# An S5/RWKV-7 layer: S5's second tables and phases on ScalarE, one scan per batch, block masks first in the queue

## The chip, the cores and the metric

The kernel runs on one core of a Trainium2 chip. The metric is the time of one execution in microseconds (us), measured on the device. The engines are called as in the profile: PE (TensorE, matmuls), DVE (VectorE), ACT (ScalarE), POOL (GpSimd), SP (SyncE, which issues most DMAs).

## The reference

One layer of a hybrid decoder, for 1024 tokens of width 1024, all in float32:

```
h    = rms_norm(x);  proj = h @ w_in
# columns: RWKV r, k, v (3 x 512), low-rank downs, S5 input u (512), two gates
o_rwkv = rwkv7_branch(...) @ w_branch_rwkv      # 8 heads of 64, a state per head, token by token
o_s5   = s5_branch(u, ...) @ w_branch_s5
x = x + rms_norm((sigmoid(gA) * o_rwkv + sigmoid(gB) * o_s5) @ w_out)
x = x + rms_norm(conv_ffn(rms_norm(x)))         # gated MLP with a causal convolution of width 3

# S5: 32 groups of 16 channels, 64 complex states per group
a_bar = exp(lam * dt);  b_bar = ((a_bar - 1) / lam) * b
s_t   = a_bar * s_(t-1) + b_bar u_t             # along the tokens
y     = Re(c s) + d u;  then gelu and a sigmoid gate

# RWKV-7: the state S of a head, per token
S = S * w + (S a) b^T + v k^T;   y = S r        # a = -kk, b = kk * sigmoid(..)
```

## The kernel before

**Products.** A float32 product is split: each operand is a rounded part and a remainder, and three matmuls of 128x512 (L172, L173, L174) give hi*hi, lo*hi and hi*lo for each k tile of 128. A weight tile is loaded by SP (wf, L155), rounded on ACT (wh, L156), and its remainder is made on DVE (wl, L157).

**Order of the work.** PE's order is the order in which the program emits its matmuls. `drive` (L179) runs lanes: generators that yield what their PE work costs and when (or on what condition) they may go on. When no lane is due, `background` emits a step of the projections in the fill list (input projections, r, k and v, gates), whose matmuls fill PE while the lanes' small operations run elsewhere. The order on the other engines comes from a scheduler that takes instructions by priority: the lanes' number (HP, the more urgent HP2, and HPW, more urgent still, which weight loads and projections have).

**S5 stage** (`drive` at L1785, lanes `s5_lane` and `tab_lane`). The 32 groups are worked in 4 batches of 8 groups; time is cut into 128 blocks of 8 tokens, so a batch's tiles are 128 partitions x 8 groups x 128 blocks (the 128 partitions hold the real part of the 64 states in one half, the imaginary part in the other). `s5_tables(b)` (L492) makes the tables of a batch from step powers: the input side bb, bw, bx (small tiles of 128x128; `lin` is two products and a sum, L508 to L510), from bw and bx the table w, and the output side ca and cb (`tab`, L529; sums at L532 and L537). w is transposed on PE (L544) and copied (L545, L546); the short convolution kpad is multiplied on PE (L553), copied (L554) and unrolled into toep by 8 DMAs (L562). Then it makes the phases: block number times frequency, in a high and a low part fh and fl (L569, L572), reduced by whole turns (L570, L571, L574, L575), and then |x| (L576) and two sines (L577, L578), which give the cosine cs and the sine sn.

`s5_batch(b)` (L583) multiplies the input by the transposed table into two PSUM tiles p1, p2 (L598), turns them by cs and sn (L600 to L602), runs along the blocks the recurrence z = rho * z + rot with one scan per group (L605, 8 scans of 127 columns, each from zero), turns the state (L607, L608), and PE adds three products per group: toep with u (L613), ca with z (L614), cb with rot (L615). The PSUM tiles called chk, two in number, serve all of L544, L553, L598 and L613 to L615. A copy (L616) and a DMA end the batch. All wide tiles come from one pool (t4).

**RWKV stage** (`drive` at L1795ff, four lanes). Heads are worked in pairs; a front (`rwkv_front`, L639) takes the two pairs u = 0, 1 of a group g for one half th of the tokens. `prep_lane(0)` and `prep_lane(1)` run the fronts g = 0 (here "the first front") and g = 1 ("the second front") of each token half; with g = 1 the inverses follow. A front loads k, tz, ta, r, v (L654, from a pool `ld` of ten tiles); squares k (L669) and scans the decay (L673); makes bk1 (L674, L675); sums the squares on PE (L680) into a tile of the PSUM pool rp, which has two; from these the inverse square (L684, L685) and yb (L686); the exponentials pe and tz (L690, L691); the operands ar0, bk0 (L693 to L695); transposes yb on PE into kb (L700); bk0, ar1, r and bk1 (L703 to L706); and then, for each pair and each half q of its eight chunks, 16 block products on PE (L718, 64x128) into two of the four PSUM buffers cz, which two multiplications by a mask empty into gr (L721). L725 makes the bonus product, L730 and L737 DMA the results out on POOL's queue. `rwkv_nat` (L740) transposes bk (L747) and v (L762) and copies them on ACT (L754, L756, L767); its eight-fold V copies free rp. `chain_lane` then runs the level (L822) and the chain.

The second front of a half begins when the first has masked its first pair (`masked`), and its own instructions go on when T_LD has passed (`start`), in the second token half for g = 0 when the first chain is done.

## Time and profile before

| | |
|---|---|
| three runs | 1543.03, 1545.65, 1549.22 us (median 1545.65) |
| the profiled execution | 1545.26 us |
| its span, first to last instruction | 1543.5 us, so 1.8 us lie around it |
| granted PE clock, mean over the span | 0.974 |
| busy: PE / DVE / ACT / POOL | 1455.5 / 1084.8 / 696.9 / 74.0 us |
| S5 stage | about 84 to 262 us |
| first two RWKV fronts | about 262 to 345 us |
| fronts of the second token half | about 500 to 560 us |

A row of the waits names the waiting instruction's output and line, the instruction that released it, and the sum, the number and the longest of these waits. A row of the groups names line, engine, operation, output and input with their shapes, then busy time and mean ns, then the idle time in front of them. A timeline row has start, length, engine, line and operation, and in brackets the idle time before it with its releaser. In the windows the granted clock is the share of full speed that the throttle gave PE in that stretch.

### The profile page before, as it was taken

Reading aid. Unit: us, or ns where it says so; the run is one execution under the profiler, and the core shown is the slowest. Engines: PE = TensorE matmul, PEld = TensorE weight load, DVE = VectorE, ACT = ScalarE, POOL = GpSimd, SP = SyncE. Lnnn points to the kernel's source line nnn. Section 1 sums busy time; section 2 is a strip of 40 time slices with the busy share of each in tenths; the row PEclk is TensorE's granted clock in tenths of the full one; section 3 lists DMA queues with packets and bytes.
Section 4 is the critical chain, followed back from the end, with each engine's and each line's share of the span. In section 5 each row is a group of like instructions: output and inputs, shape, how many; then the busy total and the mean of one; then the engine's idle time right before and its main releaser. Section 6 shows DMA issues by size and latency. Waiting matters only on the chain.

```text
span 1543.5 us, 24191 instructions
## 1 busy us (share of the span) xinstructions
PE 1455.5 (94%) x9332; PEld 1191.3 (77%) x9332; DVE 1084.8 (70%) x1783; ACT 696.9 (45%) x1077; POOL 74.0 (5%) x126
## 2 busy tenths in 40 slices
PE   5999899999999899899898999999999999999996
PEld 4788788778777677678676888788888887888785
DVE  6898784845325748466587689777777777698777
ACT  5364442533324535436444446444444444443451
POOL 2100000001100010000100000000000000000001
PEclk9999999999999899999998999999999999999998
DMA  6164242623511475424864444322222225953632
GB/s 209 42 205 126 87 127 100 206 88 117 158 57 63 152 225 161 119 79 132 269 217 153 151 144 133 111 83 82 82 82 82 82 85 195 335 169 114 214 109 109
DMA packets 130339, 210.45 MB, mean 136 GB/s; under 512 B 37696, under 2 KB 43840, under 8 KB 130224
## 3 DMA queue, kind: packets, MB, share of 16 engines
q1 hardware_dynamic: 122480, 185.17, 37.4%
q0 software_dynamic: 6592, 21.64, 4.1%
q10 hardware_dynamic: 1152, 2.10, 0.4%
q8 instruction: 73, 1.20, 0.3%
q14 instruction: 42, 0.34, 0.1%
HBM read 153.28 MB, written 53.48 MB: 134 GB/s over the span
## 4 chain that ended last, share of the span: by engine, by line
PE 76%; DVE 10%; DMA 6%; ACT 4%; issue 3%; SPq 0%; POOL 0%; ACTq 0%; DVEq 0%; POOLq 0%
PE gm L172 9%; PE gm L173 8%; PE gm L174 8%; PE rp L1384 4%; PE d L1559 4%; PE d L1558 4%; PE rp L1385 4%; PE rp L1386 4%; PE d L1560 4%; PE mm L1384 2%; PE mm L1386 2%; PE mm L1385 2%; PE ch L172 1%; PE ch L173 1%; PE ch L174 1%
## 5 line engine op out<-in xcount | busy, mean ns | idle before, releaser
L172 PE MATMUL gm<-hh,wh 128*128 128x512 f32 x688 | 282.8, 411 | 11.1 <-DVE hl L1116 5.8
L173 PE MATMUL gm<-hl,wh 128*128 128x512 f32 x688 | 271.9, 395 | 0.2 <-DVE hl L227 0.2
L174 PE MATMUL gm<-hh,wl 128*128 128x512 f32 x656 | 258.4, 394 | 0.0
L156 ACT CAST wh<-wf 128x512 fp32r<-128x512 f32 x179 | 110.8, 620 | 225.0 <-PE gm L173 138.0
L157 DVE TENSOR_TENSOR wl<-wf,wh 128x512 fp32r<-128x512 f32 x175 | 120.2, 688 | 120.6 <-ACT wh L156 112.7
L172 PEld LDWEIGHTS gm<-hh,wh 128*128 128x128 f32 x688 | 130.8, 190 | 45.1 <-DVE hl L1116 7.5
L173 PEld LDWEIGHTS gm<-hl,wh 128*128 128x128 f32 x688 | 130.9, 190 | 25.7 <-issue 1.0
L174 PEld LDWEIGHTS gm<-hh,wl 128*128 128x128 f32 x656 | 124.9, 190 | 27.3
L1559 PE MATMUL d<-xl,wh 128*128 128x512 f32 x308 | 120.8, 392 | 3.0 <-DVE xl L227 3.0
L1558 PE MATMUL d<-xh,wh 128*128 128x512 f32 x308 | 121.1, 393 | 2.4 <-ACT xh L226 2.1
L1560 PE MATMUL d<-xh,wl 128*128 128x512 f32 x308 | 120.5, 391 | 0.0
L1384 PE MATMUL rp<-t,h 128*128 128x512 f32 x216 | 84.4, 391 | 1.4 <-ACT p L1398 1.4
L1386 PE MATMUL rp<-t,l 128*128 128x512 f32 x216 | 84.2, 390 | 0.5 <-DVE l L227 0.5
L1385 PE MATMUL rp<-t,h 128*128 128x512 f32 x216 | 84.1, 389 | 0.0
L1558 PEld LDWEIGHTS d<-xh,wh 128*128 128x128 f32 x308 | 58.2, 189 | 15.9 <-ACT xh L226 2.5
L1559 PEld LDWEIGHTS d<-xl,wh 128*128 128x128 f32 x308 | 58.2, 189 | 15.8 <-DVE xl L227 3.9
L1560 PEld LDWEIGHTS d<-xh,wl 128*128 128x128 f32 x308 | 58.2, 189 | 12.3
L226 ACT CAST h<-r 128x1024 fp32r<-128x1024 f32 x34 | 35.9, 1054 | 61.1 <-PE rp L1385 32.5
L227 DVE TENSOR_TENSOR l<-r,h 128x1024 fp32r<-128x1024 f32 x34 | 41.6, 1225 | 29.2 <-ACT h L226 27.7
L1405 DVE SCALAR_TENSOR_TENSOR y<-zv,vecs,y 128x1023 f32<-128x1023 f32 (+1 forms) x36 | 46.1, 1281 | 8.5 <-ACT y L1403 8.5
L1384 PEld LDWEIGHTS rp<-t,h 128*128 128x128 f32 x216 | 40.5, 188 | 10.8 <-ACT p L1398 2.2
L1386 PEld LDWEIGHTS rp<-t,l 128*128 128x128 f32 x216 | 40.5, 188 | 9.4 <-DVE l L227 1.0
(462 smaller groups left out, 3201.3 us busy)
## 6 DMA issues: line engine op xcount, KB each, us to landing
r<-in_w_up_dram SPq DMA_DIRECT2D x36, 512.0 KB, 3.6
wf<-in_w_in_dram SPq DMA_DIRECT2D x68, 256.0 KB, 2.9
st<-in_w_down_dram SPq DMA_DIRECT2D x55, 256.0 KB, 4.2
st<-ACT SPq DMA_DIRECT2D x44, 256.0 KB, 4.8
wf<-in_w_up_dram SPq DMA_DIRECT2D x36, 256.0 KB, 2.6
ACT<-y POOLq DMA_DIRECT2D x18, 512.0 KB, 2.9
GT<-ev SPq DMA_DIRECT2D x32, 256.0 KB, 2.4
wf<-in_w_br_dram SPq DMA_DIRECT2D x32, 256.0 KB, 3.4
```

What stands on the lines that cost most here:

```text
L156: nc.scalar.copy(h[:, :n], f[:, :n])
L157: nc.vector.tensor_tensor(l[:, :n], f[:, :n], h[:, :n].bitcast(F32), ALU.subtract)
L172: mm(ps, a, xh[k], start=k == 0, stop=False)
L173: mm(ps, a, xl[k], start=False, stop=False)
L174: mm(ps, b, xh[k], start=False, stop=k == n - 1)
L1384: mm(ps, wh[:, c], xh, start=first and k == 0, stop=False, skip_group_check=True)
L1385: mm(ps, wh[:, c], xl, start=False, stop=False, skip_group_check=True)
L1386: mm(ps, wl[:, c], xh, start=False, stop=k == 3, skip_group_check=True)
L1405: V.scalar_tensor_tensor(y[:, lag:], z[:, 0:1024 - lag], self.vec(nme, i), y[:, lag:], ALU.mult, ALU.add)
L1558: mm(ps, wh[:, c], xh[:, x], start=start, stop=False, skip_group_check=True)
L1559: mm(ps, wh[:, c], xl[:, x], start=False, stop=False, skip_group_check=True)
L1560: mm(ps, wl[:, c], xh[:, x], start=False, stop=stop, skip_group_check=True)
```

## The change

1. **Second tables.** bx and cb are bw and ca with the two halves of the partitions exchanged and one of them negated. They are now made so on ACT, two instructions each (64 partitions each); the six DVE operations per batch that made them from the inputs go, and one tile (ct2) with them.
2. **Phases.** The two 1024-wide DVE products of block number and frequency become 16 ACT activations of 128x128 with a scale per partition. After the sines, ph is filled with rho (an ACT copy) and its column 0 of every group with zero (a POOL memset), and is kept for the scan.
3. **One scan.** The turned input is written one column to the right, with column 0 zero, and one scan of 1024 columns runs over all eight groups; the zeros of ph restart it at each group.
4. **Priorities in S5.** `s5_lane` gets HP2 for HP.
5. **Fronts.** The exponentials move ahead of the first yield, the -0.5 goes into yb, and ar0, ar1, r * bk1, bk1 * tz, tz * k and bk0 are made before the kb transposes, so that one operation per pair stands behind them. The number of operations stays. T_BK is 4 for 5.
6. **Masks and the second front.** The masks get priority HPW. A counter `grams` counts fronts whose block products are all emitted; the second front's own instructions wait for that of the first (`grams > 2 * th`) in place of T_LD, and prep_lane(1) starts only when the last projection of r, k, v has begun (`all_in`).

PE has 6405 rows of instructions before and after, SP 703; DVE 1719 for 1752, ACT 1053 for 1025, POOL 111 for 106. PE's order is the same up to the first RWKV front.

In the S5 stage, batch 0, before, on ACT (t tiles: phase, sine and cosine; ev: evictions of projections; wh: weight casts):

```order
L1015 ACTIVATE ev_1416<-gm_1403,hb_a_217 128x512
L156 CAST wh_1473<-wf_1475 128x512
L576 ACTIVATE t_289_1227<-t_291_1229 128x1024
L156 CAST wh_1660<-wf_1662 128x512
L979 ACTIVATE ev_1462<-gm_1339,mu_211 128x512
L1015 ACTIVATE ev_1483<-gm_1419,hb_a_217 128x512
L1015 ACTIVATE ev_1499<-gm_1486,hb_a_217 128x512
L577 ACT_TABLE_LOAD
L577 ACTIVATE t_290_1228<-t_291_1229 128x1024
L578 ACTIVATE t_289_1227<-t_289_1227,hpi 128x1024
L1015 ACT_TABLE_LOAD
```

And after (L566 the narrow activations, L572 to L574 what was L576 to L578, L575 rho's copy):

```order
L156 CAST wh_1472<-wf_1474 128x512
L566 ACTIVATE t_287_1223<-csts,s5fl 128x128
L572 ACTIVATE t_286_1222<-t_288_1224 128x1024
L573 ACT_TABLE_LOAD
L573 ACTIVATE t_287_1223<-t_288_1224 128x1024
L574 ACTIVATE t_286_1222<-t_286_1222,hpi 128x1024
L156 CAST wh_1675<-wf_1677 128x512
L976 ACTIVATE ev_1461<-gm_1350,mu_211 128x512
L1012 ACT_TABLE_LOAD
L1012 ACTIVATE ev_1482<-gm_1425,hb_a_217 128x512
L1012 ACTIVATE ev_1498<-gm_1485,hb_a_217 128x512
L575 COPY t_288_1224<-s5rho 128x1024
```

The two sines now stand directly on the Abs, and the cast and evictions that stood between them come behind.

The same batch on DVE, before, from the end of the phase to the turned state:

```order
L984 SCALAR_TENSOR_TENSOR ev_1462<-last,vecs,ev_1462 128x1
L600 TENSOR_TENSOR t_317_1353<-chk_1426,t_289_1227 128x1024
L601 TENSOR_TENSOR t_342_1444<-chk_1427,t_290_1228 128x1024
L602 TENSOR_TENSOR t_317_1353<-t_317_1353,t_342_1444 128x1024
L605 SCALAR_TENSOR_TENSOR t_316_1351<-s5rho,t_317_1353 128x127
L980 SCALAR_TENSOR_TENSOR ev_1525<-gm_1479,vecs,ev_1525 128x511
L982 COPY last<-gm_1479 128x1
L605 SCALAR_TENSOR_TENSOR t_316_1351<-s5rho,t_317_1353 128x127 x7
L607 TENSOR_TENSOR t_317_1353<-t_316_1351,t_290_1228 128x1024
L157 TENSOR_TENSOR wl_1667<-wf_1668,wh_1666 128x512
L608 TENSOR_TENSOR t_316_1351<-t_316_1351,t_289_1227 128x1024
```

And after:

```order
L571 TENSOR_TENSOR t_288_1224<-t_288_1224,t_286_1222 128x1024
L600 TENSOR_TENSOR t_336_1450<-chk_1433,t_287_1223 128x8x127
L599 TENSOR_TENSOR t_314_1363<-chk_1432,t_286_1222 128x8x127
L157 TENSOR_TENSOR wl_1676<-wf_1677,wh_1675 128x512
L977 SCALAR_TENSOR_TENSOR ev_1461<-gm_1350,vecs,ev_1461 128x511
L981 SCALAR_TENSOR_TENSOR ev_1461<-last,vecs,ev_1461 128x1
L601 TENSOR_TENSOR t_314_1363<-t_314_1363,t_336_1450 128x8x127
L602 SCALAR_TENSOR_TENSOR t_313_1362<-t_288_1224,t_314_1363 128x1024
L603 TENSOR_TENSOR t_314_1363<-t_313_1362,t_287_1223 128x1024
L604 TENSOR_TENSOR t_313_1362<-t_313_1362,t_286_1222 128x1024
```

One scan (L602) stands for eight, and a weight remainder and an eviction now stand ahead of the sum (L601).

In the first fronts, on DVE, before (L721, gr from cz, are the first front's masks; ld, bk and ar tiles numbered from 2867 on are the second front's):

```order
L721 TENSOR_TENSOR gr_2593<-cz_2827,csts 128x4x128
L705 TENSOR_TENSOR ld_2954<-ld_2954,bk_591_2868 128x512
L721 TENSOR_TENSOR gr_2593<-cz_2828,csts 128x4x128
L706 TENSOR_TENSOR bk_591_2868<-bk_591_2868,ld_2876 128x8x64
L695 SCALAR_TENSOR_TENSOR bk_591_2868<-bk_591_2868,vecs,ld_2876 128x8x64
L157 TENSOR_TENSOR wl_3151<-wf_3152,wh_3150 128x512
L704 TENSOR_TENSOR ar_2867<-ld_2957,gr_2869 128x8x64
L693 SCALAR_TENSOR_TENSOR bk_591_2868<-ld_2882,ld_2874 128x8x64
L705 TENSOR_TENSOR ld_2957<-ld_2957,bk_591_2868 128x512
L695 SCALAR_TENSOR_TENSOR bk_591_2868<-bk_591_2868,vecs,ld_2878 128x8x64
L706 TENSOR_TENSOR bk_591_2868<-bk_591_2868,ld_2878 128x8x64
L721 TENSOR_TENSOR gr_2593<-cz_2902,csts 128x4x128
```

And after (masks L717; ld_2982, ld_2984, ar_2973 and bk_593 are the second front's):

```order
L669 SCALAR_TENSOR_TENSOR ld_2982<-csts,ld_2982 128x512
L669 SCALAR_TENSOR_TENSOR ld_2984<-csts,ld_2984 128x512
L688 SCALAR_TENSOR_TENSOR ar_2973<-ld_2978,vecs,gr_2975 128x8x64
L717 TENSOR_TENSOR gr_2609<-cz_2831,csts 128x4x128
L717 TENSOR_TENSOR gr_2609<-cz_2832,csts 128x4x128
L674 TENSOR_TENSOR bk_593_2974<-bk_593_2974,ld_2978 128x8x64
L717 TENSOR_TENSOR gr_2609<-cz_2851,csts 128x4x128
L717 TENSOR_TENSOR gr_2609<-cz_2852,csts 128x4x128
L977 SCALAR_TENSOR_TENSOR ev_2874<-gm_2793,vecs,ev_2874 128x511
L979 COPY last<-gm_2793 128x1
L674 TENSOR_TENSOR bk_593_2974<-bk_593_2974,ld_2980 128x8x64
L688 SCALAR_TENSOR_TENSOR ar_2973<-ld_2980,vecs,gr_2975 128x8x64
```

Before, eight operations of the second front and a weight remainder stand between the third mask shown and its forerunner; after, the masks follow on two scans and one product, with single operations between the first pairs of masks.

On PE, behind the first front, before (L680 are the second front's sums of squares, L747 and L762 the first front's transposes):

```order
L174 MATMUL gm_2982<-hh_319,wl_2977 128x512
L680 MATMUL rp_2998<-csts,gr_2869 128x2 x4
L680 MATMUL rp_3003<-csts,gr_2869 128x2 x4
L172 MATMUL gm_2982<-hh_324,wh_2976 128x512
L173 MATMUL gm_2982<-hl_325,wh_2976 128x512
L174 MATMUL gm_2982<-hh_324,wl_2977 128x512
L747 MATMUL cz_3037<-csts,bk_544_2592 128x128 x4
L747 MATMUL cz_3038<-csts,bk_544_2592 128x128 x4
L762 MATMUL rp_3041<-csts,ld_2789 128x128 x4
L747 MATMUL cz_3039<-csts,bk_544_2592 128x128 x4
L747 MATMUL cz_3040<-csts,bk_544_2592 128x128 x4
```

And after (L679, L744, L759):

```order
L174 MATMUL gm_2969<-hh_319,wl_2964 128x512
L744 MATMUL cz_3024<-csts,bk_532_2608 128x128 x4
L744 MATMUL cz_3025<-csts,bk_532_2608 128x128 x4
L759 MATMUL rp_3028<-csts,ld_2808 128x128 x4
L744 MATMUL cz_3026<-csts,bk_532_2608 128x128 x4
L744 MATMUL cz_3027<-csts,bk_532_2608 128x128 x4
L759 MATMUL rp_3029<-csts,ld_2811 128x128 x4
L679 MATMUL rp_3074<-csts,gr_2975 128x2 x4
L679 MATMUL rp_3079<-csts,gr_2975 128x2 x4
```

The sums of squares now follow directly on the transposes, with no projection between.

The diff, without the setting up of the new counters and the handing on of ph:

```diff
     lin(bw, bre, bc_c(s["w3"]), bim, bc_c(s["w4"]), ALU.add, V)
-    lin(bx, bre, bc_c(s["w4"]), bim, bc_c(s["w3"]), ALU.subtract, V)
+    A.mul(bx[HALF[0]], bw[HALF[1]], -1.0)
+    A.copy(bx[HALF[1]], bw[HALF[0]])
 
...
     V.tensor_tensor(ca, ca, ct, ALU.add)
-    ct2 = self.s5p.tile([128, 8, 9, 16], F32, tag="ct", name=self.nm("ct"))
-    tab(V, cb, cre, s["q2"], 1)
-    tab(V, ct2, cim, s["q1"], 1)
-    V.tensor_tensor(cb[:, :, 1:9, :], cb[:, :, 1:9, :], ct2[:, :, 1:9, :], ALU.subtract)
+    A.copy(cb[HALF[0], :, 1:9, :], ca[HALF[1], :, 1:9, :])
+    A.mul(cb[HALF[1], :, 1:9, :], ca[HALF[0], :, 1:9, :], -1.0)
 
...
     cs, sn, ph = self.t4(shape=(128, 8, 128)), self.t4(shape=(128, 8, 128)), self.t4(shape=(128, 8, 128))
-    nrow = self.cst("nrow").unsqueeze(1).to_broadcast([128, 8, 128])
-
-    def bc_n(x):
-        return x[:, g8].unsqueeze(2).to_broadcast([128, 8, 128])
-    V.tensor_tensor(ph, nrow, bc_n(s["fh"]), ALU.mult)
+    for t, f in ((ph, s["fh"]), (sn, s["fl"])):
+        for g in range(8):
+            A.activation(t[:, g], self.cst("nrow"), AF.Identity, scale=f[:, b * 8 + g:b * 8 + g + 1])
     V.tensor_scalar(cs, ph, MAGIC, -MAGIC, ALU.add, ALU.add)
     V.tensor_tensor(ph, ph, cs, ALU.subtract)
-    V.tensor_tensor(sn, nrow, bc_n(s["fl"]), ALU.mult)
     V.tensor_tensor(ph, ph, sn, ALU.add)
...
     A.activation(cs, cs, AF.Sin, bias=self.hpi, scale=-SIN_SCALE)
+    A.copy(ph, s["rho"][:, g8].unsqueeze(2).to_broadcast([128, 8, 128]))
+    G.memset(ph[:, :, 0:1], 0.0)
 
...
     z = self.t4(shape=(128, 8, 128))
-    G.memset(z[:, :, 0:1], 0.0)
     rot = self.t4(shape=(128, 8, 128))
+    G.memset(rot[:, :, 0:1], 0.0)
     yield 0, T_US
...
     r2 = self.t4(shape=(128, 8, 128))
-    V.tensor_tensor(rot, p1, cs, ALU.mult)
-    V.tensor_tensor(r2, p2, sn, ALU.mult)
-    V.tensor_tensor(rot, rot, r2, ALU.add)
-    for g in range(8):
-        gg = b * 8 + g
-        V.tensor_tensor_scan(z[:, g, 1:128], s["rho"][:, gg:gg + 1].to_broadcast([128, 127]),
-                             rot[:, g, 0:127], 0.0, ALU.mult, ALU.add)
+    lead, turn = (slice(None), slice(None), slice(0, 127)), rot[:, :, 1:128]
+    V.tensor_tensor(turn, p1[lead], cs[lead], ALU.mult)
+    V.tensor_tensor(r2[lead], p2[lead], sn[lead], ALU.mult)
+    V.tensor_tensor(turn, turn, r2[lead], ALU.add)
+    V.tensor_tensor_scan(*(t.rearrange("p g n -> p (g n)") for t in (z, ph, rot)), 0.0, ALU.mult, ALU.add)
     V.tensor_tensor(rot, z, sn, ALU.mult)
...
         V.tensor_tensor_scan(tz, self.cst("smask"), tz, 0.0, ALU.mult, ALU.add)
+        G.memset(e["pe"][:, :, 0:1], 1.0)
+        A.activation(e["pe"][:, :, 1:65], c64(tz), AF.Exp, scale=-0.5 * CDEC)
+        A.activation(tz, tz, AF.Exp, scale=0.5 * CDEC)
         A.activation(e["bk1"], c64(e["ta"]), AF.Identity, bias=self.ka_1[:, p:p + 1], scale=self.ka_h[:, p:p + 1])
...
         V.reciprocal(y, y)
-        A.copy(c64(e["yb"]), y.unsqueeze(2).to_broadcast([128, 8, 64]))
+        A.mul(c64(e["yb"]), y.unsqueeze(2).to_broadcast([128, 8, 64]), -0.5)
     for e in L:
         p, tz = e["p"], e["tz"]
-        G.memset(e["pe"][:, :, 0:1], 1.0)
-        A.activation(e["pe"][:, :, 1:65], c64(tz), AF.Exp, scale=-0.5 * CDEC)
-        A.activation(tz, tz, AF.Exp, scale=0.5 * CDEC)
-        A.copy(pt[:, :, p], e["pe"][:, :, 64])
-        V.scalar_tensor_tensor(e["bk0"], c64(e["ta"]), 1.0, c64(e["k"]), ALU.add, ALU.mult)
         V.scalar_tensor_tensor(e["ar0"], c64(e["k"]), self.vec("k_k", p), e["pe"][:, :, 0:64], ALU.mult, ALU.mult)
-        V.scalar_tensor_tensor(e["bk0"], e["bk0"], self.vec("k_k", p), c64(tz), ALU.mult, ALU.mult)
+        V.tensor_tensor(e["ar1"], c64(e["r"]), e["pe"][:, :, 1:65], ALU.mult)
+        V.tensor_tensor(c64(e["r"]), c64(e["r"]), e["bk1"], ALU.mult)
+        V.tensor_tensor(e["bk1"], e["bk1"], c64(tz), ALU.mult)
+        V.tensor_tensor(tz, tz, e["k"], ALU.mult)
+        V.scalar_tensor_tensor(e["bk0"], c64(e["ta"]), 1.0, c64(tz), ALU.add, ALU.mult)
+        A.copy(pt[:, :, p], e["pe"][:, :, 64])
     yield 0.6, T_KN, 1.5
...
     for e in L:
-        r, tz = e["r"], e["tz"]
-        V.scalar_tensor_tensor(e["bk0"], e["bk0"], -0.5, c64(e["kb"]), ALU.mult, ALU.mult)
-        V.tensor_tensor(e["ar1"], c64(r), e["pe"][:, :, 1:65], ALU.mult)
-        V.tensor_tensor(c64(r), c64(r), e["bk1"], ALU.mult)
-        V.tensor_tensor(e["bk1"], e["bk1"], c64(tz), ALU.mult)
+        V.scalar_tensor_tensor(e["bk0"], e["bk0"], self.vec("k_k", e["p"]), c64(e["kb"]), ALU.mult, ALU.mult)
         e["v"] = ld(self.RKV[8 + e["p"]])
...
                            stop=True, skip_group_check=True)
-            for h in range(2):
-                V.tensor_tensor(d["gr"][:, u, 4 * q:4 * q + 4, h], ps[h], gm, ALU.mult)
+            with self.tc.high_priority(HPW):
+                for h in range(2):
+                    V.tensor_tensor(d["gr"][:, u, 4 * q:4 * q + 4, h], ps[h], gm, ALU.mult)
         if u:
...
                                         d["gr"][q:q + 32, :, :, h, 32 * blk:32 * blk + 32].rearrange("p u c t -> p (u c) t"))
+            self.grams += 1
         else:
...
     for mt in (4 + p, p, 8 + p):
+        self.all_in = mt > 8 and p == 3
         def use(th, ps):
...
-            self.drive([(HP, self.s5_lane()), (HP, self.tab_lane())])
+            self.drive([(HP2, self.s5_lane()), (HP, self.tab_lane())])
...
     for th in range(2):
-        yield 0, (lambda: self.masked >= 2 * th + 1) if g else (lambda: self.chunks >= 14 * th)
+        yield 0, (lambda: self.masked >= 2 * th + 1 and self.all_in) if g else (lambda: self.chunks >= 14 * th)
         d = self.ds[th][g]
         self.rwkv_tiles(d, g, th)
-        yield from self.rwkv_front(d, g, th, self.pts[th], (lambda: self.chains >= 1) if th > g else T_LD)
+        yield from self.rwkv_front(d, g, th, self.pts[th], (lambda: self.chains >= 1) if th > g else (lambda: self.grams > 2 * th) if g else T_LD)
         self.fronts += 1
...
-T_KN, T_BK, T_GR, T_NF, T_MT, T_INV, T_LV, T_CH = 7.0, 5.0, 4.0, 5.0, 8.0, 43.0, 1.0, 0.8
+T_KN, T_BK, T_GR, T_NF, T_MT, T_INV, T_LV, T_CH = 7.0, 4.0, 4.0, 5.0, 8.0, 43.0, 1.0, 0.8
```

More of the change, by code (lines that the diff above doesn't have):

```diff
@@ L578, in s5_tables @@
         A.activation(cs, cs, AF.Sin, bias=self.hpi, scale=-SIN_SCALE)
-        d.update(ca=ca, cb=cb, cs=cs, sn=sn, toep=toep, wT=wT)
+        A.copy(ph, s["rho"][:, g8].unsqueeze(2).to_broadcast([128, 8, 128]))
+        G.memset(ph[:, :, 0:1], 0.0)
+        d.update(ca=ca, cb=cb, cs=cs, sn=sn, toep=toep, wT=wT, ph=ph)
         yield 1.8, T_TRIG
@@ L587, in s5_batch @@
         mm = nc.tensor.matmul
-        ca, cb, cs, sn, toep, wT = (d[n] for n in ("ca", "cb", "cs", "sn", "toep", "wT"))
+        ca, cb, cs, sn, toep, wT, ph = (d[n] for n in ("ca", "cb", "cs", "sn", "toep", "wT", "ph"))
         u8 = self.u8[b]
         z = self.t4(shape=(128, 8, 128))
-        G.memset(z[:, :, 0:1], 0.0)
         rot = self.t4(shape=(128, 8, 128))
+        G.memset(rot[:, :, 0:1], 0.0)
         yield 0, T_US
@@ L685, in rwkv_front @@
             V.reciprocal(y, y)
[L686 removed]
+            A.mul(c64(e["yb"]), y.unsqueeze(2).to_broadcast([128, 8, 64]), -0.5)
         for e in L:
             p, tz = e["p"], e["tz"]
[L689 to L691 removed]
+            V.scalar_tensor_tensor(e["ar0"], c64(e["k"]), self.vec("k_k", p), e["pe"][:, :, 0:64], ALU.mult, ALU.mult)
+            V.tensor_tensor(e["ar1"], c64(e["r"]), e["pe"][:, :, 1:65], ALU.mult)
[3 more added lines that the diff above has]
+            V.scalar_tensor_tensor(e["bk0"], c64(e["ta"]), 1.0, c64(tz), ALU.add, ALU.mult)
             A.copy(pt[:, :, p], e["pe"][:, :, 64])
[L693 to L695 removed]
         yield 0.6, T_KN, 1.5
@@ L1758, in front_half @@
         self.mark, self.chained = False, False
-        self.s5_in_done, self.stored, self.mixed_in, self.open = -1, None, False, 0
+        self.s5_in_done, self.stored, self.mixed_in, self.all_in, self.open = -1, None, False, False, 0
         with tc.tile_pool(name="lxp", bufs=4) as self.lxp, tc.tile_pool(name="s5c", bufs=1) as self.s5c, \
@@ L1794, in front_half @@
             self.ds = [[{}, {}], [{}, {}]]
+            self.grams = 0
             self.fronts, self.masked, self.preps, self.chains, self.chunks, self.outs, self.z = 0, 0, 0, 0, 0, 0, {}
```

1 line of the change is left out of this document (removed).

## The prediction

> **What bounds the kernel now.** The page's busy line and clock line come first.
>
> ```profile
> PE 1455.5 (94%) x9332; PEld 1191.3 (77%) x9332; DVE 1084.8 (70%) x1783; ACT 696.9 (45%) x1077; POOL 74.0 (5%) x126
> ...
> PEclk9999999999999899999998999999999999999998
> ```
>
> TensorE works 94% of the span, in an order written by hand, and its instructions stay as many. So only its waits, and the clock lost behind them, can be won or lost here. The second view is the list of PE's waits (waiting instruction, what released it, total us, times, longest), cut to the S5 stage, the first two RWKV fronts, and the fronts of the second token half:
>
> ```profile
> PE chk L614 <- DVE t L608: 6.3, 2, 4.1
> PE chk L544 <- DVE t L600: 1.3, 1, 1.3
> PE chk L553 <- DVE t L601: 0.7, 1, 0.7
> ```
> ```profile
> PE cz L718 <- DVE gr L721: 5.5, 3, 4.4
> PE gm L172 <- ACT wh L156: 1.8, 1, 1.8
> ```
> ```profile
> PE cz L747 <- ACT bk L756: 2.6, 1, 2.6
> PE rp L680 <- DVE ld L736: 1.9, 2, 1.6
> PE rp L762 <- DVE sv L684: 1.2, 1, 1.2
> PE rp L700 <- DVE bk L703: 1.1, 1, 1.1
> PE rp L918 <- ACT V L767: 0.7, 1, 0.7
> PE rp L700 <- ACT ld L922: 0.5, 1, 0.5
> ```
>
> In S5, 8.3 us end with VectorE's work on the scanned states; in the first fronts 5.5 us end with the masks that empty the four block-product buffers; in the second half 8.0 us have many causes. The third view, windows, shows the clock (stretch, length, PE, PEld, DVE, ACT and POOL busy, then the granted clock):
>
> ```profile
> 100.00:136.00 36.00, 35.86 (x185) 29.84 (x184) 30.40 (x45) 23.64 (x33) 0.84 (x1) 1.00 0.52 164
> 136.00:150.00 14.00, 11.79 (x76) 10.76 (x77) 13.42 (x22) 4.13 (x5) 0.11 (x1) 0.88 0.31 81
> 172.00:192.00 20.00, 13.94 (x81) 12.23 (x81) 15.48 (x24) 7.90 (x11) 0.00 (x0) 0.83 0.22 66
> 262.00:300.00 38.00, 36.16 (x217) 29.91 (x219) 24.97 (x45) 19.04 (x32) 1.76 (x7) 0.96 0.61 208
> 300.00:318.00 18.00, 12.51 (x107) 8.37 (x99) 15.92 (x27) 3.14 (x7) 1.26 (x2) 0.81 0.29 93
> 518.00:545.00 27.00, 19.04 (x98) 15.13 (x97) 18.41 (x33) 16.19 (x37) 4.85 (x8) 0.81 0.52 157
> ```
>
> The clock loss is length times missing clock: 14 x 0.12 = 1.7, 20 x 0.17 = 3.4, 18 x 0.19 = 3.4, 27 x 0.19 = 5.1 us. These come on top of the waits.
>
> [...] The window 262 to 300 holds one wait, of 1.8 us, and loses 38 x 0.04 = 1.5 us of clock. [...]
>
> **S5, VectorE.**
>
> ```profile
> L605 DVE TENSOR_TENSOR_SCAN t<-s5rho,t 128x127 f32<-128x127 f32 x32 | 10.5, 400 | 0.1
> ...
> L572 DVE TENSOR_TENSOR t<-csts,s5fl 128x1024 f32<-128x1024 f32 x4 | 4.9, 1219 | 0.0
> ...
> L537 DVE TENSOR_TENSOR cb<-cb,ct 128x1024 f32<-128x1024 f32 x4 | 4.9, 1215 | 0.0
> ...
> L510 DVE TENSOR_TENSOR sml<-sml,sml 128x128 f32<-128x128 f32 x9 | 2.5, 283 | 0.0
> ```
> ```profile
> DMA to landing us min/median/max: 2.3/3.9/5.7
> L673 DVE TENSOR_TENSOR_SCAN ld<-csts,ld x4: 1199/1221/1226, 277.2 to 297.2; 128x512 f32<-128x512 f32 x4
> ```
>
> Per batch go three small products of bx (3 x 0.28 = 0.85), three 1024-wide operations of cb (3.65) and two of the phases (2.4). Eight scans, 10.5/4 = 2.6 us per batch, become one of 1024 columns. No row shows that width; two of 512 columns (L673) bound it above at 2.44, the eight narrow ones at 2.6, and I take 2.4. VectorE loses about 7 us per batch.
>
> **S5, ScalarE.** It gains 16 narrow activations, two halves of cb, two of bx and the copy of rho.
>
> ```profile
> L1015 ACT ACTIVATE ev<-gm,hb_a 128x512 f32<-128x512 f32 x8 | 5.3, 689 | 0.9 <-PE gm L174 0.9
> ...
> L545 ACT COPY wT<-chk 128x1024 f32<-128x1024 f32 x4 | 4.0, 1012 | 1.6 <-PE chk L544 1.6
> ...
> L754 ACT COPY bk<-cz 128x256 f32<-128x256 f32 x4 | 1.5, 371 | 0.1
> ...
> L692 ACT COPY pt<-gr 128x8 f32<-128x8 f32 x4 | 0.8, 194 | 0.0
> ```
>
> A 128x128 activation lies between the 128x8 copy (0.19) and the 128x256 copy (0.37), or 0.69 if a scale column makes it like L1015; I take 0.28, so 4.5 us, with 3.1 to 11 as ends. The two cb halves and rho are 1.0 each (L545), the bx halves 0.28 each: 8 us per batch. In the 36 us from 100 to 136 ScalarE has 12.4 free, so it fits; at 0.69 (14.6 us) it does not.
>
> [...]
>
> What matters is when the cosine is ready. Batch 0, first VectorE, then ScalarE:
>
> ```profile
> 122.74 1.23 DVE L575 TENSOR_TENSOR t<-t,t 128x1024 f32<-128x1024 f32 x1
> ...
> 135.68 2.29 DVE L605 TENSOR_TENSOR_SCAN t<-s5rho,t 128x127 f32<-128x127 f32 x7
> ...
> 139.82 1.22 DVE L608 TENSOR_TENSOR t<-t,t 128x1024 f32<-128x1024 f32 x1
> ```
> ```profile
> 116.75 0.61 ACT L156 CAST wh<-wf 128x512 fp32r<-128x512 f32 x1
> 124.00 1.06 ACT L576 ACTIVATE t<-t 128x1024 f32<-128x1024 f32 x1 [6.63 <-DVE t L575]
> ...
> 127.33 1.28 ACT L577 ACT_TABLE_LOAD   x1
> ...
> 129.59 1.14 ACT L578 ACTIVATE t<-t,hpi 128x1024 f32<-128x1024 f32 x1
> ```
>
> Now L608 ends at 141.0, 2.2 after PE wanted it, so at 138.8. In the changed order the last narrow piece follows the cast of 116.75 and is done at 117.7; three VectorE operations (1.2, 0.7, 1.2) bring the phase to about 121.1, not 124.0. The Abs, the table load and the two sines then stand side by side (1.06 + 1.28 + 1.06 + 1.14): cosine at 125.6, not 130.7. Behind it stand on VectorE two rotations, a weight remainder that waits for a cast, an eviction and the sum; the scan also waits for rho's copy, behind a table load and two evictions on ScalarE (to about 130.6), and a POOL memset. The scan ends at 133.1, the two products at 135.6: 3.2 us before PE asks. Gone are 2.2 + 1.7.
>
> Batch 1: the sines were split by another activation and two table loads.
>
> ```profile
> 170.46 1.28 ACT L996 ACT_TABLE_LOAD   x1
> ...
> 173.70 1.15 ACT L578 ACTIVATE t<-t,hpi 128x1024 f32<-128x1024 f32 x1
> ```
>
> From 170.46 to 173.70 that is 3.2 us, out of the new order; VectorE's lost work ahead of the phase is worth about 4 more. All 7 us earlier and 3.9 for batch 0, its last product ends near 173.8; PE wants it at 184.9 - 4.1 - 2.0 - 3.9 = 174.9. [...] Gone are 1.3 + 0.7 + 4.1 + 3.4. Batches 2 and 3 show no wait now and get more room. S5: 8.3 + 1.7 + 3.4 = **13.4 less**.
>
> **First fronts.** The masks of the first front now stand behind the second front's two scans and one product, not behind about ten of its operations. The block products come at 297.8 and 303.9; the scans wait for loads that land near 299, so masks run at 301 to 304 and the buffers are free in time: 5.5 + 3.4 = 8.9 less. A wait appears: the second front's sums (new L679) follow directly on the transposes whose two rp buffers ScalarE empties with four copies of about 0.37 each (L754 is the nearest row). PE reaches them some 1.6 before those 3 us of copies end. I take +1.6 without clock loss; with it, +3.2, without a wait 0. First fronts: **7.3 less** (from 1 to 8.9).
>
> A second cost hides there: r of the second front takes a buffer that the first front's product leaves by a POOL DMA. From 310.4, two transfers of 2.3 to 5.7 bring r at 315 to 322, ten operations of 0.7 make it 322 to 329, and PE wants the products near 330. Cost nothing, slack 1 to 8. The wait of 1.8 on a weight cast at 270 stays: nothing that it hangs on is edited. The operations moved ahead of the kb transposes keep their number and their 0.7 each; behind the transposes one of VectorE's stays per pair instead of four, so T_BK's shorter due time (18 projection matmuls of filling between transposes and products, not 24) finds the operand ready. The all_in condition and HP2 add no instruction; what they reorder on VectorE is in the walk above.
>
> **Second half.** The same moves, but its waits mostly lie on ScalarE's copies and on sv. Walking the new order I find waits of 1.1, 1.5, 1.0, 0.8, 0.7 and some smaller, about 8 again, with 3 of clock for 5.1: **2 less**, between 13.1 less (all waits and clock gone) and 3 more.
>
> **The sum.** 13.4 + 7.3 + 2 = 22.7 from the profiled execution's 1545.26 is 1522.6, say **1523**. That execution lies 0.4 below the median of the runs, 1545.65.
>
> **The rivals.**
> 1. The masks still come late: the scans ahead of them wait for a load that lands at the 5.7 end, 2 to 4 us later. The 4.4 wait stays for the most part. Then only S5 counts, with the second half's 2 and a part of the first fronts: 1545.3 - 13.4 - 1 = 1531. For it: both scans do stand ahead. Against it: the load is issued before the products.
> 2. Batch 1 is only shortened: ScalarE's halves of cb and small tables come late, VectorE waits for them, and the 4.1 wait keeps 2 with its 3.4 of clock. 1523 + 5 to 10 = 1528 to 1533.
> 3. The change does not do what it says: at 0.69 a piece, 11 us of narrow pieces end batch 0's phase 6.4 us later than I have it, so the cosine is at 132, no earlier than before; projections' evictions and casts queue behind them and PE waits there instead. S5's gain is spent, and with only part of the first fronts' left the time is 1540 to 1545. It decides from about 0.48 us a piece, where 16 x 0.2 use up batch 0's margin of 3.2.
> 4. Slower: r's load of the second front. Behind it on SP's queue stand the weight loads of the next projections, on VectorE the whole second front. If the buffer comes free so late that r lands after 323, PE waits one for one at the second block products, in both halves. At 15 us late it costs 2 x 15 and 2 x 3.4 of clock, less the gain of 22.7: 1545 + 14 = 1559. Against it: the transfer rows stop at 5.7.
>
> **How the numbers follow.** Forecast 0.52 (1516 to 1528, the bounds of its terms), rival 1 0.15, rival 2 0.12, rival 3 0.11, rival 4 0.10. A measurement of this kernel tells about 0.5% from no change: below 1538 is faster, above 1553 slower. Forecast and rivals 1 and 2 are faster, 0.79; rival 3 is the same, 0.11; rival 4 is slower, 0.10. The range starts at 1512, where the second half loses most of its 13, and ends at 1544, inside rival 3.
>
> **What would show it.** Right: no wait of PE on L604 (before L608), L544 or L553 between 120 and 262 and a clock of 1.00 there; no wait on the masks at 300; a wait of 1 to 2 us at L679 about 320. The narrow pieces read 0.25 to 0.4 each, the scan 2.3 to 2.5. Wrong: narrow pieces over 0.48, PE waiting for ScalarE's evictions or casts in S5, or the second block products waiting for r.

## The result and the profile after

The changed kernel takes 1536.82 us (median of 5 runs, 1531.40 to 1538.08), the kernel before 1547.59 (5 runs, 1543.03 to 1549.22) beside it. The ratio is 0.9931, with a 95% interval of 0.9910 to 0.9953: 10.8 us faster by the medians. A second measurement of both kernels, beside the last experiments, gave 0.9954 (0.9938 to 0.9970), 6.5 us. The sign was as forecast; the size is just under half of the 22.7 us of the sum, and in the second measurement under a third. The profiled execution took 1538.08 us, the longest of its five, with a span of 1536.3, 7.2 shorter than that of before. All of PE's waits together fell from 76.1 to 68.4 us between the two profiles; the granted clock over the whole span is 0.974 in both, so in this pair the gain is waiting alone.

Lines of the changed kernel are up to four lower than in the kernel before (L717 for L721, L679 for L680, L1012 for L1015). PE's waits between 84 and 345 us, so in the S5 stage and the first two fronts:

```profile
PE gm L172 <- ACT ev L1012: 4.4, 1, 4.4
PE rp L679 <- DVE sv L683: 3.2, 1, 3.2
PE gm L172 <- DVE last L979: 1.8, 1, 1.8
PE rp L679 <- ACT V L764: 0.9, 1, 0.9
PE cz L713 <- DVE gr L717: 0.3, 2, 0.2
```

Every S5 wait of before is gone (8.3 us on L608, L600 and L601), and of the 5.5 on the masks 0.3 is left. In their place stand two new ones: 4.4 for an eviction on ScalarE in S5, and 3.2 + 0.9 for the PSUM tiles of the second front's sums. The 1.8 is the wait of before; it has another releaser's name now. In the second half, 8.0 us of waits became 5.7:

```profile
PE rp L915 <- ACT ld L919: 1.9, 2, 1.1
PE rp L915 <- ACT V L764: 1.6, 2, 0.9
PE rp L679 <- DVE ld L733: 0.9, 1, 0.9
PE rp L699 <- DVE bk L701: 0.8, 1, 0.8
PE rp L759 <- DVE sv L683: 0.5, 1, 0.5
```

The windows of the same places (stretch, length, busy PE, PEld, DVE, ACT, POOL, then the granted clock):

```profile
124.00:140.00 16.00, 11.63 (x45) 9.13 (x44) 10.84 (x12) 10.87 (x13) 0.95 (x2) 0.89 0.30 93
258.00:300.00 42.00, 39.72 (x290) 31.68 (x288) 31.34 (x56) 20.54 (x36) 1.51 (x7) 1.00 0.61 200
300.00:322.00 22.00, 17.86 (x83) 14.95 (x82) 12.69 (x25) 10.39 (x25) 3.76 (x6) 0.77 0.38 109
405.00:425.00 20.00, 16.68 (x393) 13.58 (x387) 3.55 (x5) 7.48 (x19) 0.00 (x0) 0.66 0.31 113
514.00:541.00 27.00, 21.25 (x102) 16.77 (x101) 20.10 (x36) 16.47 (x37) 4.84 (x8) 0.81 0.62 186
```

Length times missing clock is 1.8 us at the S5 wait, none at the wait of 1.8, 5.1 at L679, 6.8 at the start of the chain, 5.1 in the second half. In the kernel before it was 1.7 + 3.4 in S5, 1.5 + 3.4 in the first fronts and 3.5 at the start of the chain (0.86 in 400 to 425). What S5 won in clock, 3.3, was lost again at the start of the chain.

**Where the S5 wait comes from.** ScalarE in batch 0 of the changed kernel:

```profile
119.97 0.61 ACT L156 CAST wh<-wf 128x512 fp32r<-128x512 f32 x1
120.48 0.40 ACT L566 ACTIVATE t<-csts,s5fl 128x128 f32<-128x128 f32 x1
124.46 1.06 ACT L572 ACTIVATE t<-t 128x1024 f32<-128x1024 f32 x1 [3.58 <-DVE t L571]
125.54 1.28 ACT L573 ACT_TABLE_LOAD   x1
126.84 1.06 ACT L573 ACTIVATE t<-t 128x1024 f32<-128x1024 f32 x1
127.80 1.13 ACT L574 ACTIVATE t<-t,hpi 128x1024 f32<-128x1024 f32 x1
128.84 0.60 ACT L156 CAST wh<-wf 128x512 fp32r<-128x512 f32 x1
129.35 0.68 ACT L976 ACTIVATE ev<-gm,mu 128x512 f32<-128x512 f32 x1
130.04 1.28 ACT L1012 ACT_TABLE_LOAD   x1
131.34 1.26 ACT L1012 ACTIVATE ev<-gm,hb_a 128x512 f32<-128x512 f32 x2
```

The Abs starts at 124.46; before it was 124.00. So the phase, the thing that the change hurries, is no earlier at all. And from 124.46 on ScalarE runs an undivided block: Abs, table load, two sines, then a cast, another eviction and the load of the other table, 6.9 us in all, before the eviction at 131.34, for which PE has stood since 127.7:

```profile
132.08 0.50 PE L172 MATMUL gm<-lx,wh 128*128 128x512 f32 x1 [4.37 <-ACT ev L1012]
```

In the kernel before, a cast and three evictions ran between the Abs and the sines.

**Where the wait at L679 comes from.** VectorE at the first fronts:

```profile
294.20 1.28 DVE L717 TENSOR_TENSOR gr<-cz,csts 128x512 f32<-128x512 f32 x2
...
299.78 2.47 DVE L717 TENSOR_TENSOR gr<-cz,csts 128x512 f32<-128x512 f32 x4
...
310.04 0.69 DVE L689 TENSOR_TENSOR ar<-ld,gr 128x512 f32<-128x512 f32 x1 [5.20 <-DMA ld<-RKV]
...
313.43 0.16 DVE L683 TENSOR_SCALAR sv<-rp 128x8 f32<-128x8 f32 x1
```

The masks come at 294 to 302, early enough. Then VectorE stands for 5.2 us for the load of r, because L689 is next in its queue. Behind it, five operations later, stands the small L683 (0.16 us) that empties the first sums; PE's second sums wait for just that. (The first sums were ready at 310.4, 3.0 us before L683 ran.)

### The profile page after: what moved, and what is told of

It is laid out like the page before. It is cut to its first block, busy times and chain, and to the rows that moved or that the text cites. A ratio compares the mean times of both kernels' runs of the same rounds, so it can differ in the third digit from the quotient of the medians.

```text
span 1536.3 us, 24215 instructions
## 1 busy us (share of the span) xinstructions
PE 1455.9 (95%) x9332; PEld 1193.2 (78%) x9332; DVE 1061.0 (69%) x1723; ACT 730.2 (48%) x1161; POOL 74.8 (5%) x130
## 5 line engine op out<-in xcount | busy, mean ns | idle before, releaser
L172 PE MATMUL gm<-hh,wh 128*128 128x512 f32 x688 | 285.9, 416 | 13.6 <-DVE hl L1114 7.6
L1556 PE MATMUL d<-xh,wh 128*128 128x512 f32 x308 | 120.9, 393 | 2.1 <-ACT xh L226 2.1
L1396 ACT COPY p<-rp 128x512 f32<-128x512 f32 x54 | 31.0, 574 | 37.0 <-PE rp L1384 37.0
```

The costliest lines, as they stand in the source:

```text
L172: mm(ps, a, xh[k], start=k == 0, stop=False)
L1556: mm(ps, wh[:, c], xh[:, x], start=start, stop=False, skip_group_check=True)
```

## The experiments

My theory after the result, **A**: both new waits are displaced ones. In S5 the undivided block holds up evictions; at the first fronts the late r holds up L683. Rivals: **B**, the gain is handed back by later stages; **C**, only one part of the change gains; **D**, the r wait comes only with S5's earlier end (**D2** is another rival: L683 is late for its place in the queue, whatever r does); **E**, the moved operations are needed where the change put them; **F**, ScalarE has simply too much work. Each ratio is against the kernel before on the same chip, with its 95% interval.

**One part alone.** The diff's hunks up to the scan and `s5_lane`'s priority, and the rest.

```diff
+            A.mul(bx[HALF[0]], bw[HALF[1]], -1.0)
...
+                self.drive([(HP2, self.s5_lane()), (HP, self.tab_lane())])
```

for the first (all hunks of `s5_tables` and `s5_batch` between these), and for the second all others:

```diff
+            G.memset(e["pe"][:, :, 0:1], 1.0)
...
+T_KN, T_BK, T_GR, T_NF, T_MT, T_INV, T_LV, T_CH = 7.0, 4.0, 4.0, 5.0, 8.0, 43.0, 1.0, 0.8
```

> The kernel before with the S5 part of the change alone (tables, phases, one scan, the lane's priority). Theory A (the S5 waits on L608, L544 and L553 are gone, but the Abs, table load and two sines that now stand side by side on ScalarE hold up the evictions behind them): the trace shows one wait of about 4.4 us of a projection on ScalarE's L1012 near 128 and one slow stretch of 3.4 us behind it, S5 ends 7 us earlier than before, and the whole is 6 to 8 us faster (ratio 0.995). Rival B (what S5 wins is given back at the chain and the norms, which wait for other engines): S5 ends 7 earlier, the whole is only 2 to 4 faster. Rival C (most of the 10.8 comes from the fronts): under 3 faster, with S5 ending less than 4 earlier.

Measured: 0.9975 (0.9957 to 0.9992), about 4 us faster. The waits of 84 to 345 us:

```profile
PE cz L714 <- DVE gr L717: 4.8, 2, 4.4
PE gm L172 <- ACT ev L1011: 4.3, 1, 4.3
PE gm L172 <- DVE last L978: 1.8, 1, 1.8
```

The S5 part brings its own eviction wait and leaves the mask wait, as A has it. S5 ends 7.5 us earlier than before (its last product at 255.3 for 262.8), as A and B both have it. The gain by the medians, 4.6 us, lies between A's 6 to 8 and B's 2 to 4, and the interval, 1.2 to 6.6 us, reaches into both.

> The kernel before with the RWKV part alone (operands moved, masks ranked first, second front waits). Theory A (the mask waits of 5.5 are gone, but the second front's sums wait 4.1 for rp: 0.9 for ScalarE's V copies, 3.2 for VectorE's L683, which stands in the queue behind operations that wait for r's load): the same two waits at L679, a slow stretch of 6.8 to 10.2, and with the second half's 2 the whole is 2 to 5 faster (ratio 0.997 to 0.999). Rival C: 8 or more faster. Rival D (the r wait comes only from the earlier end of S5, by which the loads of the stage are pressed together): here no wait on L683, and 7 or more faster.

Measured: 0.9983 (0.9967 to 1.0000), some 2.6 us.

```profile
PE rp L683 <- DVE sv L687: 2.6, 1, 2.6
...
PE rp L683 <- ACT V L768: 0.9, 1, 0.9
```

The wait on sv is there without the S5 part (lines are four higher here), so D falls. C wanted 8 us or more here; the interval ends at 5.1, so C falls too. It also touches 1.0000, so the times alone do not show that this part gains. The two parts together give 0.9958, and the change itself 0.9931 and 0.9954: within the intervals they add up.

**r's load.** Two ways to free it of the first front's transfer.

The first, at the end of `rwkv_front`, leaves out the bonus product of pb and v and sends v in its place, so that r's tile comes free when PE has read it:

```diff
-            V.tensor_tensor(e["r"], e["pb"], e["v"], ALU.mult)
-            nc.gpsimd.dma_start(d["bv"][u], e["r"])
+            nc.gpsimd.dma_start(d["bv"][u], e["v"])
```

The second moves three operations behind the kb transposes again:

```diff
-            V.tensor_tensor(e["ar1"], c64(e["r"]), e["pe"][:, :, 1:65], ALU.mult)
-            V.tensor_tensor(c64(e["r"]), c64(e["r"]), e["bk1"], ALU.mult)
-            V.tensor_tensor(e["bk1"], e["bk1"], c64(tz), ALU.mult)
-            V.tensor_tensor(tz, tz, e["k"], ALU.mult)
+            V.tensor_tensor(e["k"], tz, e["k"], ALU.mult)
...
             V.scalar_tensor_tensor(e["bk0"], e["bk0"], self.vec("k_k", e["p"]), c64(e["kb"]), ALU.mult, ALU.mult)
+            V.tensor_tensor(e["ar1"], c64(e["r"]), e["pe"][:, :, 1:65], ALU.mult)
+            V.tensor_tensor(c64(e["r"]), c64(e["r"]), e["bk1"], ALU.mult)
+            V.tensor_tensor(e["bk1"], e["bk1"], c64(e["tz"]), ALU.mult)
```

> The changed kernel, but the bonus product of pb and v is left out and v is sent in its place, so that r's tile comes free when PE has read it, and the second front's load of r no longer waits for a transfer. Theory A: VectorE's idle time of 5.2 before L689 falls to under 2, L683 runs when its sums are there, the wait of 3.2 at L679 goes and with it half or more of the slow stretch of 10.2: 4 to 7 faster than the changed kernel, 1530 to 1533. Rival D2 (L683 is late for its place in the queue, whatever r does): the wait stays over 2 and the time within 2 of the changed kernel's.

Measured: 0.9941 (0.9914 to 0.9967). VectorE's idle time before L689 is 2.1 us for 5.2, and the wait on sv 1.1 for 3.2:

```profile
304.54 0.69 DVE L689 TENSOR_TENSOR ar<-ld,gr 128x512 f32<-128x512 f32 x1 [2.08 <-DMA ld<-RKV]
```
```profile
PE rp L679 <- DVE sv L683: 1.1, 1, 1.1
PE rp L679 <- ACT V L763: 0.9, 1, 0.9
```

The wait moved with r's load, as A has it, and D2's mark (over 2) is missed. The time did not follow clearly: the ratio lies between the change's own two, 0.9931 and 0.9954. One reason stands in the second half, where the wait at the kb transposes (L699, on L701) is 3.0 us for 0.8 in the change.

> The changed kernel with the three operations that need r (ar1, r x bk1, bk1 x tz) behind the kb transposes, as before, and tz x k written over k; the pool then gives the second front's r a tile that waits for VectorE alone, not for the first front's product to be sent. Nothing is left out. Theory A: as with the bonus product left out, the 3.2 at L679 falls under 1.5, 3 to 6 faster than the changed kernel (1531 to 1534). Rival D2: no faster. Rival E (the operations behind kb are needed where they were moved): the wait at L679 goes and one of 1 to 3 us comes at the block products L713.

Measured: 0.9932 (0.9909 to 0.9955). At L679 it does what A says, the clock there is 0.93 in 295 to 320 (1.8 us lost, not 5.1; but a second trace of the change, shown at the end, also lost only 1.8):

```profile
PE rp L679 <- ACT V L764: 0.9, 1, 0.9
PE rp L679 <- DVE sv L683: 0.5, 1, 0.5
```

But here too the time did not follow. In the second half, where the same edit applies, a wait at the transposes (L696) appears, rival E's kind, one step earlier than I put it:

```profile
PE rp L696 <- DVE bk L698: 3.3, 1, 3.3
```

So the cure was tried in the first half alone, with the three operations ahead of the transposes under the first condition and behind them under the second:

```diff
+            if th:
...
+            if not th:
```

> The changed kernel with the operations that need r behind the kb transposes in the first token half alone; the second half as in the change. Theory A: up to 405 as with both halves moved (L679 waits 0.9 and 0.5, a slow stretch of 3.4 to 6.8), and after 500 as in the change (waits of about 6 us, none of 3.3 at the kb transposes): 4 to 7 faster than the changed kernel. Rival B (what is won before 400 is given back by the waits of the chain and the norms after 600): under 2 faster, with those waits longer by as much.

Measured: 0.9901 (0.9873 to 0.9928). L679 waits 0.9 and 0.7, and the second half is as in the change. The three kernels of the next section, measured beside it, gave nearly the same ratio, and the change itself was not measured with them, so none of these four times says by itself what a cure is worth; the waits do, and the times of the last four runs.

**The block on ScalarE.**

Three edits, each by itself: the phases' products on VectorE again, the Abs on VectorE, and the low-rank products after every fourth step of `mix_in`.

```diff
-            for g in range(8):
-                A.activation(t[:, g], self.cst("nrow"), AF.Identity, scale=f[:, b * 8 + g:b * 8 + g + 1])
+            V.tensor_tensor(t, self.cst("nrow").unsqueeze(1).to_broadcast([128, 8, 128]),
+                            f[:, g8].unsqueeze(2).to_broadcast([128, 8, 128]), ALU.mult)
```
```diff
-        A.activation(cs, ph, AF.Abs)
+        V.scalar_tensor_tensor(cs, ph, -1.0, ph, ALU.mult, ALU.max)
```
```diff
-        yield from mixed(self.rkv(0), self.lowrank(xs[0], ((0, "w0", self.TZ), (1, "a0", self.TA))), 3)
+        yield from mixed(self.rkv(0), self.lowrank(xs[0], ((0, "w0", self.TZ), (1, "a0", self.TA))), 4)
```

> The changed kernel with the phases made on VectorE again (two wide products in place of 16 narrow activations), all else as changed. Theory A (the new wait of 4.4 comes from the undivided block of Abs, table load and two sines, not from the narrow pieces): the block stays together, the wait on ScalarE's evictions near 125 stays between 3 and 5, and the time is within 3 of the changed kernel's. Rival F (ScalarE is overfilled by the pieces): the wait falls under 1.5 and S5 ends 3 or more earlier than in the changed kernel.

Measured: 0.9905 (0.9874 to 0.9936); the wait is 1.5, at the edge of what F wanted (under 1.5) and well below A's 3 to 5. S5 ends at 250.2, 5.8 us earlier than in the change, which is F's mark too (3 or more).

```profile
119.29 1.06 ACT L572 ACTIVATE t<-t 128x1024 f32<-128x1024 f32 x1 [2.10 <-DVE t L571]
120.37 1.28 ACT L573 ACT_TABLE_LOAD   x1
121.66 1.06 ACT L573 ACTIVATE t<-t 128x1024 f32<-128x1024 f32 x1
122.63 1.14 ACT L574 ACTIVATE t<-t,hpi 128x1024 f32<-128x1024 f32 x1
123.67 1.03 ACT L575 COPY t<-s5rho 128x1024 f32<-128x1024 f32 x1
```

The block is as undivided as before, and has even rho's copy in it, but it stands 5.2 us earlier, and PE's wait behind it shrinks. That corrects A: the wait is also a matter of when the block comes. The 16 narrow pieces, strewn between evictions that go first, end at 120.9 and make the phase 5.2 us later than two VectorE products do. So far F is right: between 95 and 121 ScalarE is busy for 25.65 of the 26 us (16.55 in the kernel before). It has free time again only behind the last piece, 3.58 us just ahead of the Abs.

> The changed kernel with the Abs of the phase on VectorE (one operation of 1.2 beside the table load) in place of ScalarE's activation of 1.06. Theory A: the block on ScalarE is 1.06 shorter and the wait at 127 falls from 4.4 to about 3.3; S5 ends 1 us earlier, whole 1 faster, less than the runs tell apart. Rival F: the wait stays at 4.4 within 0.3.

Measured: 0.9897 (0.9869 to 0.9925); the wait is 3.3 for 4.4, the 1.06 by which the block is shorter. The block theory's number is hit. S5 does not end 1 us earlier, as expected, but 0.5 later. A clock loss of 3.4 us behind the wait, twice the 1.7 of the change, would account for that; this is an estimate from the 1.5 us between the two. The whole is not told apart from its neighbours.

> The changed kernel with the low-rank products, of one k tile each and an eviction each, strewn among the r, k, v products after every fourth step, not every third. Nothing is left out; TensorE's order changes between 90 and 150. Theory A (evictions that come every few steps fill the four gm buffers while ScalarE is in its block): with fewer evictions due in those 7 us, and two of them ahead of the block in the order, the wait falls from 4.4 to under 2 and S5 ends 3 to 6 earlier: 1528 to 1534 beside a changed kernel of 1535. Rival F: the wait stays over 3.

Measured: 0.9898 (0.9872 to 0.9924). The S5 wait is gone; the list for 84 to 345 is

```profile
PE rp L679 <- DVE sv L683: 2.6, 1, 2.6
PE gm L172 <- DVE last L979: 1.8, 1, 1.8
PE rp L679 <- ACT V L764: 0.9, 1, 0.9
```

The order on ScalarE:

```profile
121.43 1.06 ACT L572 ACTIVATE t<-t 128x1024 f32<-128x1024 f32 x1 [0.70 <-DVE t L571]
122.40 0.60 ACT L156 CAST wh<-wf 128x512 fp32r<-128x512 f32 x1
122.90 0.72 ACT L1014 ACTIVATE ev<-ev,ones 128x512 f32<-128x512 f32 x1
123.64 1.28 ACT L573 ACT_TABLE_LOAD   x1
```

The pieces are still on ScalarE, but with fewer evictions due the Abs starts 3.0 us earlier, a cast and one more operation stand between it and the sines, and nothing waits. So F's load on ScalarE alone does not make the wait: it takes the late block and the evictions due behind it. S5 ends at 249.7, 13.1 us earlier than in the kernel before.

**Both cures together, beside the change.** Four kernels on one chip; their edits are those above, joined:

> The changed kernel as it stands, once more, for comparison with the three below on the same chip. Theory A: PE's waits are those of its first profile within 0.5 us in S5 and the first fronts (4.4 on ScalarE's eviction, 0.9 and about 3 at L679); the slow stretches after 400 may lie otherwise. The whole is 6 to 14 faster than the kernel before.

> Phases on VectorE and, in the first token half, the operations that need r behind the transposes: both cures in one kernel, the rest as changed. Theory A: the S5 wait is about 1.5 without a slow stretch, L679 waits 0.9 and under 1, and the whole is 4 to 10 faster than the changed kernel (two waits of 2.9 and 2.3 less and two slow stretches of 3.4 less). Rival B (given back later): no more than 2 faster, the waits at L819 and after 600 longer by as much.

> The low-rank products strewn after every fourth step and, in the first token half, the operations that need r behind the transposes; the phases stay on ScalarE. Theory A: no S5 wait, L679 waits 0.9 and under 1, 6 to 12 faster than the changed kernel. Rival B: no more than 2 faster.

> All three: phases on VectorE, low-rank products after every fourth step, r behind the transposes in the first token half. Theory A: no S5 wait either, so the same as with the phases on ScalarE and every fourth step, within 2. Rival F (the narrow pieces cost time beyond the one wait): 3 or more faster than that one.

| kernel | median us | ratio to before (interval) | S5 wait on ScalarE | L679: V copies, sv |
|---|---|---|---|---|
| the change, again | 1536.86 | 0.9954 (0.9938 to 0.9970) | 4.4 | 0.9, 2.3 |
| phases on VectorE + r behind kb in the first token half | 1527.31 | 0.9887 (0.9861 to 0.9913) | 1.5 | 0.9, 0.7 |
| every fourth step + r behind kb in the first token half | 1524.16 | 0.9866 (0.9844 to 0.9888) | 0 | 0.9, 0.7 |
| all three | 1526.52 | 0.9887 (0.9866 to 0.9908) | 0 | 0.9, 0.3 |

The third beats both kernels: 12.7 us below the change and 19.2 below the kernel before (1543.39 beside it). Two reservations: the spans of the two profiled executions, the change's and this one's, differ by 8.5 (1530.9 and 1522.4), and 12.7 is a little more than A's 6 to 12. Small waits on the masks came back with the cures, 0.7, 1.1 and 1.7 us in the three kernels. PE's clock was full through the S5 block and lost 1.8 us at the fronts:

```profile
120.00:140.00 20.00, 20.00 (x121) 17.19 (x120) 14.71 (x21) 15.21 (x21) 0.95 (x2) 1.00 0.45 152
...
295.00:320.00 25.00, 23.34 (x119) 19.46 (x118) 16.02 (x31) 12.35 (x28) 3.75 (x6) 0.93 0.47 143
```

B falls: what the cures win stays won. F's last claim falls too, since the fourth kernel is not faster than the third (it is 2.4 slower, where A had within 2; the intervals overlap).

Not run: the two reorderings in the kernel before. What they would be worth without the change stays open, so the 19.2 is the worth of the change with them, and not of the change alone.

## Why the prediction was right in sign and half in size

- **VectorE's savings were right.** The one scan takes 2.29 us (I took 2.4), and every wait on the scanned states is gone.
- **ScalarE's prices were right, its timetable was not.** A narrow piece takes 0.39 us alone and three in a row 0.97, so about 0.3 each; I had taken 0.28. cb's halves take 1.05, rho 1.03:

```profile
L566 ACT ACTIVATE t<-csts,s5fl 128x128 f32<-128x128 f32 x32 | 10.1, 387 | 0.0
...
L535 ACT COPY cb<-ca 64x1024 f32<-64x1024 f32 x4 | 4.2, 1048 | 1.9 <-DVE ca L534 1.8
```

- **The step that failed in S5** is "the last narrow piece follows the cast of 116.75 and is done at 117.7". It was done at 120.9, since the cast itself had slipped: the same cast ran at 119.97. I set the new instructions into the old times of their neighbours and took the 12.4 us that ScalarE had free between 100 and 136 as room for them. But 6.6 of these lay behind that cast; from 95 to 117.4, ahead of the phase, only 5.8 were free, and the new work there (5.6 for the 16 pieces, 4.2 for the cb halves of two batches) takes 9.8. From it follow the phase at 124.4 (I had 121.1), the cosine at 128.9 (125.6), and the last product at 138.5 (135.6). PE asked for it at 145.1, but only because the new wait and the clock behind it had made PE 6.2 late; without them it would have been just in time.
- **The step that was missing in S5:** I counted the four instructions standing side by side as a gain for the cosine, and did not ask what queues behind them. That is 4.4 us of wait and 1.8 of clock, which takes 6.2 off the 13.4: the profile shows 7.2 (waits 8.3 to 4.4, clock 5.1 to 1.8). It is rival 3's place with another cause, a block that came late, not pieces that are dear. Without this wait the sum for S5 was nearly right: with the products after every fourth step S5 ends 13.1 us earlier, where I had 13.4.
- **The masks were right** (5.5 became 0.3), and so was the new wait on the V copies, though I priced it at 1.6 and it is 0.9.
- **The step that failed at the first fronts** is "Cost nothing, slack 1 to 8" for r's late load. The load itself came about when I said (310.0 here, 317 with S5's 7 us added back; I had 315 to 322). I asked only whether the block products would wait for r. They did not; L683, which needs no r, was in the queue behind the operations that do. That cost 3.2, and 5.1 of clock was lost there, where I had counted it gone. Of 7.3 forecast, the profile shows 1.1 less waiting (7.3 to 6.2 with the 1.8 in it) and no less clock lost, for 4.9 became 5.1. (In the second trace of the change the wait on L683 was 2.3 and the clock lost 1.7 + 1.8.)
- **The second half was right in size by luck:** 2.3 us less waiting (8.0 to 5.7) with the clock loss equal at 5.1. I had 2 the other way round: waits of about 8 again, and 2 less of clock.
- **The clock terms** were nearly half of the sum: 5.1 in S5, 3.4 at the first fronts and 2 in the second half, 10.5 of 22.7. In the profiled pair the 3.3 of clock won in S5 was lost again elsewhere, and over the whole span nothing of the 10.5 is left (0.974 both times).
- **With both displaced waits cured** the kernel gains 19.2 of the 22.7 us. So the mechanism of the gain was right for the most part. What took it away lay in the places of rivals 3 and 4, to which I gave a fifth of the chance, but by other causes than theirs: the pieces are not dear, and the block products did not wait for r.

What stays open: why the wait at the start of the chain (L819, 2.9 to 4.3 us in the kernels with the whole change, 2.8 in the kernel before) grows at times; the profile names no releaser there.

## What to carry to other kernels

When work moves to an engine with slack, do not lay the new instructions beside the old times: write that engine's whole new order, and let every neighbour slip. For each block that becomes undivided and each operation that waits for a load, list what stands behind it on the same engine and whom that releases; an operation of 0.16 us that stood behind a late load cost TensorE 3.2 us, though it did not need what was loaded. Count an engine's slack up to the time at which the new work is due, not over a window that reaches beyond it. And try the cure of each displaced wait by itself before giving the change its verdict: the change was worth under half of its sum, the change with two small reorderings 19.2 of 22.7 us.

## What the hardware showed that I had not expected

The clock loss behind one and the same wait was not the same in each execution. The wait of 1.8 us at the first fronts' start is in the trace of the kernel before and in both of the change. In the kernel before, 1.5 us of clock were lost behind it (window 262 to 300, 0.96), in the first trace of the changed kernel none (window 258 to 300 above, 1.00), in the second trace of the very same kernel again 42 x 0.04 = 1.7:

```profile
258.00:300.00 42.00, 40.16 (x288) 32.27 (x287) 32.03 (x57) 20.30 (x35) 1.66 (x7) 0.96 0.60 196
300.00:322.00 22.00, 18.73 (x96) 15.87 (x95) 12.58 (x25) 11.03 (x26) 3.75 (x6) 0.92 0.40 120
400.00:425.00 25.00, 20.72 (x464) 16.56 (x462) 6.25 (x9) 7.49 (x19) 0.00 (x0) 0.80 0.35 116
```

At L679 the two executions lost 5.1 and 1.8, at the chain 6.8 and 5.0. Over the whole span the mean clock was 0.974 and 0.978, some 40 and 34 us lost; the spans, 1536.3 and 1530.9, differ by about as much. In the kernel before and in the first trace of the change the clock reads 0.50 inside each stretch of loss (before: 272.3 to 275.6 and 415.7 to 422.4; the change: 310.6 to 320.7 and 409.6 to 423.1), and the stretches are 3.4, 6.8, 10.2 or 13.7 us long, multiples of one length, but for the stretch that the end of the program cuts off. A sum that counts each clock loss at its full size in one execution carries, by these two traces, some 6 us of chance, which is about as wide as the spread of this kernel's runs (1531.40 to 1538.08).
